# First attention of a two-block transformer: queries as high over low halves in 128 rows, values as high beside low, two matmul passes in place of three

## The chip, the core and the metric

The kernel runs on one core of a Trainium2 chip. Its time is the device time of one execution in microseconds, and the number that counts is the median of several executions. A core has the engines TensorE (PE in the profile: matrix products into PSUM; its weight loads are shown apart as PEld), VectorE (DVE), ScalarE (ACT), GpSimd (POOL) and SyncE (SP, which issues the loads).

## What is computed

Two transformer blocks over 512 tokens of width 1024, all in float32. The first block has two layers; each layer mixes the tokens in three branches (an attention over all tokens, a pooling mixer, an attention over a neighbourhood) and closes with a gated feed-forward part. The second block has a convolution layer and a layer with dilated attention. The change is in the first branch, the attention over all tokens, which occurs once in each of the two layers of the first block:

```python
def global_axial_attention(q, k, v, gq, gk):
    ...
    q = rmsnorm(q.reshape(B, S, A_HEADS, HEAD_DIM), gq)        # 8 heads of 64
    k = rmsnorm(k.reshape(B, S, A_KV_HEADS, HEAD_DIM), gk)     # 2 heads of 64
    v = v.reshape(B, S, A_KV_HEADS, HEAD_DIM)
    q = rope_2d(q, row, col) * (HEAD_DIM ** -0.5)
    k = rope_2d(k, row, col)
    ...
        s = jnp.einsum('bqkgd,bskd->bkgqs', qi, k).astype(jnp.float32)
        p = jax.nn.softmax(s, axis=-1)
        return jnp.einsum('bkgqs,bskd->bqkgd', p.astype(v.dtype), v)
```

## The kernel before

All large products are made in a float32 form (`F32R`) that TensorE streams in one pass but that keeps fewer bits. Each operand is therefore split into a high part (a copy rounded to that form, made on ACT) and a low part (the operand minus the high part, made on DVE), and a product is three passes into one PSUM tile: high by high, high by low, low by high (`mm3`, lines 325 to 327, for the weights; `split_out`, lines 671 and 672, makes the two parts). The weights stream from memory in units of eight 128x128 tiles (`raw`, line 270) and are split on the chip two units ahead of their use (lines 295 and 296).

A layer of the first block begins with `mixer`. In its first stage the projections of the pooling branch, of k, of v and of the four pairs of query heads run one after the other (`pool_inputs`, `axial_inputs`), and what follows each projection runs beside the next ones. For k and each q that is `rope`: squares on ACT (`rsq`, line 739), a scaled copy on ACT (`rqg`, line 740), small sums on PE (`qks`, line 744), a rotation on PE (`rot`, line 749), a short chain of 128x8 operations on DVE (`qkv`, `nwa`, `qky`), a product on POOL (line 755), and on DVE `rrs` (line 757) and the sum into `rqg` (line 759). Then the parts are made: `kh` and `kl`, `qh` and `ql`. Before, `k` of head e (of two) stands in its own 64 partitions of a 128-partition tile whose other 64 are zero, so that `qh[:, i]`, which holds two heads one above the other, can be multiplied whole; `vh` and `vl` likewise have zeros in the other head's 64 columns.

The second stage is `axial_lane`: two lanes take sixteen units (a pair of heads i, half of the tokens u, a head e of the pair). A unit makes two score tiles of 128 queries by 512 keys (`sc`, lines 862 to 864), a softmax of each (maximum on DVE line 835, exponent on ACT line 842, reciprocal on DVE line 846, scaling on POOL line 847), four transposes of each (`pt`, line 875), a split of the result into `ph` and `pl`, and twelve products of 256 columns with v (`po`, lines 890, 893 and 894: four blocks of keys by three passes). The four units of a pair i add into one `po` tile, which is then split into `yh[:, i]` and `yl[:, i]`. Beside the lanes runs `branch(l, 1, ...)`, the gates (`mm`) and output products (`z`) of the pooling branch. After the stage the neighbourhood attention begins.

What stands next to what on an engine is decided when the program is made: each lane says how long it will wait (`AX_NEXT`, `AX_SOFTMAX`, `AX_PROB`), `spend` advances a clock with each piece of PE work, `tick` lets a lane go on when its time has come, and the layer below moves single instructions among each other. Each engine then works through its list in order. PSUM has eight tiles: three for `mm`/`z`, three (tag `a`) that `sc`, `pt` and `rot` share, two (tag `b`) for `po`, `qks` and others.

Of the kernel before, what the change touches and what calls it, by code (L numbers as in the profile page):

```python
# [226 lines left out]
class Kernel:  # L227
# [534 lines left out]
    def axial_inputs(self, l):  # L762
# [4 lines left out]
        vh = self.ap.tile([P, 4, 2, P], F32R, tag="vh", name="vh")  # L767
        vl = self.ap.tile([P, 4, 2, P], F32R, tag="vl", name="vl")
        qh = self.ap.tile([P, 4, S], F32R, tag="qh", name="qh")
        ql = self.ap.tile([P, 4, S], F32R, tag="ql", name="ql")  # L770
        rq = self.ap.tile([P, 4, 8], F32, tag="rq", name="rq")
        zero = self.rp.tile([P, S], F32, tag="wide", name="zero")
        nc.gpsimd.memset(zero, 0.0)
        none = zero[:, :256].rearrange("p (i d) -> p i d", i=4)
        for v in (vh, vl):
            nc.scalar.activation(v[:, :, 0, 64:], none, AF.Copy)
            nc.scalar.activation(v[:, :, 1, :64], none, AF.Copy)
        for k in (kh, kl):
            nc.scalar.activation(k[64:, 0], zero[64:], AF.Copy)
            nc.scalar.activation(k[:64, 1], zero[:64], AF.Copy)  # L780
        done = [False] * 4

        def on_k(ps):
# [13 lines left out]
            for e, r in ((0, slice(0, 64)), (1, slice(64, P))):  # L797
                nc.scalar.activation(kh[r, e], qg[r], AF.Copy)
                nc.vector.tensor_tensor(kl[r, e], qg[r], kh[r, e].bitcast(F32), op=OP.subtract)

        def on_v(ps):
# [8 lines left out]
            self.split_out(vh[:, :, 0, :64], vl[:, :, 0, :64], pt[:, :, :64])  # L810
            self.split_out(vh[:, :, 1, 64:], vl[:, :, 1, 64:], pt[:, :, 64:])

        def on_q(ps, i):
            qg, y = yield from self.rope(ps, self.vec(f"qk_norm_q{l}"))
            self.split_out(qh[:, i], ql[:, i], qg)
# [11 lines left out]
        return jobs, (kh, kl, vh, vl, qh, ql, rq), done  # L827
# [21 lines left out]
    def axial_lane(self, units, st, tiles, y):  # L849

        nc = self.nc
        kh, kl, vh, vl, qh, ql, rq = tiles
        yh, yl = y
        while units:
            i, u, e = units.popleft()
# [3 lines left out]
            for t in (2 * u, 2 * u + 1):  # L859
                cols = slice(t * P, (t + 1) * P)  # L860
                ps = self.psum("a", "sc")
                nc.tensor.matmul(ps, qh[:, i, cols], kh[:, e], start=True, stop=False)
                nc.tensor.matmul(ps, qh[:, i, cols], kl[:, e], start=False, stop=False)
                nc.tensor.matmul(ps, ql[:, i, cols], kh[:, e], start=False, stop=True)
                self.spend(0.65)
# [15 lines left out]
            if i not in st:  # L881
                st[i] = self.psum("b", "po")
                st[i, "n"] = 0
# [13 lines left out]
            if st[i, "n"] == 4:  # L897
                self.split_out(yh[:, i], yl[:, i], po)
# [783 lines left out]
```

## Time and profile before

| | |
|---|---|
| median of 3 runs | 3252.92 us (3252.04 to 3722.86) |
| the profiled execution | 3250.97 us |
| its span, first to last instruction | 3249.2 us |
| PE busy | 3157.3 us, 97% |
| DVE busy | 1783.0 us, 55% |
| ACT busy | 1329.3 us, 41% |
| mean granted TensorE clock | 0.992 of full speed |

The profile is of one execution. Busy times of PE count a product until its result has left the array, so products overlap in the list: what one costs is the distance from its start to the start of the next. The chain of waits is followed back from the last instruction and tells which engine held the end up. The stage of `axial_lane` lies from 91 to 223 us in the first layer and from 940 to 1072 us in the second.

### The profile page before, as it was taken

To read this page: it belongs to the slowest core of one execution; us is meant where nothing else is said; L and a number is where in the kernel's file an instruction comes from. 1 tells how busy PE (TensorE), PEld (TensorE's weight loads), DVE (VectorE), ACT (ScalarE), POOL (GpSimd) and SP (SyncE) were. 2 spreads that over 40 slices of the span, in tenths; PEclk is the share of its full clock that TensorE was granted. 3 is DMA by queue.
4 is the path that set the end of the run, shared out by engine and by line. 5 is a ranking of instruction groups with operands and counts; after the bars stand their busy time and mean duration, and the time that the engine had idled before them with its cause. 6 is when DMAs were issued, how large, how long until landed. Compare 5 with 4: busy or idle time off the path is not lost.

```text
span 3249.2 us, 41363 instructions
## 1 busy us (share of the span) xinstructions
PE 3157.3 (97%) x16172; PEld 2664.2 (82%) x16172; DVE 1783.0 (55%) x3187; ACT 1329.3 (41%) x2160; POOL 493.7 (15%) x448
## 2 busy tenths in 40 slices
PE   8999999999999999999999989999899999999998
PEld 7887888888888788888879868888788888888886
DVE  6668446456675753645465356446634454464555
ACT  5456334334444643434343154334333333353332
POOL 0113110000111322000005410000433334100001
PEclk9999999999999999999999989999999999999999
DMA  3112232222221222232232222222222222222221
GB/s 141 59 61 74 98 111 79 97 100 94 91 69 53 77 87 101 84 104 96 95 108 77 67 80 71 98 97 104 84 72 79 77 78 79 79 85 98 97 98 72
DMA packets 86403, 281.80 MB, mean 87 GB/s; under 512 B 11584, under 2 KB 17984, under 8 KB 86208
## 3 DMA queue, kind: packets, MB, share of 16 engines
q1 hardware_dynamic: 85632, 278.10, 24.7%
q8 instruction: 128, 2.10, 0.3%
q10 hardware_dynamic: 576, 1.05, 0.1%
q14 instruction: 67, 0.55, 0.1%
HBM read 274.91 MB, written 2.10 MB: 85 GB/s over the span
## 4 chain that ended last, share of the span: by engine, by line
PE 87%; DVE 8%; ACT 4%; issue 1%; DMA 0%; POOL 0%; SPq 0%; DVEq 0%; ACTq 0%; POOLq 0%
PE mm L327 18%; PE mm L326 18%; PE mm L325 18%; PE mm L511 6%; PE mm L512 6%; PE mm L513 6%; PE conv L1264 2%; ACT junk L382 2%; PE z L327 1%; PE z L326 1%; PE z L325 1%; DVE w L296 1%; PE htp L444 1%; PE pt L875 1%; PE dpo L1398 1%
## 5 line engine op out<-in xcount | busy, mean ns | idle before, releaser
L325 PE MATMUL mm<-hh,w 128*128 128x512 f32 (+1 forms) x2720 | 1052.7, 387 | 0.0
L326 PE MATMUL mm<-hl,w 128*128 128x512 f32 (+1 forms) x2720 | 1035.2, 381 | 0.0
L327 PE MATMUL mm<-hh,w 128*128 128x512 f32 (+1 forms) x2720 | 1035.0, 381 | 0.0
L296 DVE TENSOR_TENSOR w<-raw,w 128x1024 fp32r<-128x1024 f32 x436 | 567.8, 1302 | 465.7 <-ACT w L295 461.0
L327 PEld LDWEIGHTS mm<-hh,w 128*128 128x128 f32 x2720 | 511.8, 188 | 96.5 <-issue 1.2
L326 PEld LDWEIGHTS mm<-hl,w 128*128 128x128 f32 x2720 | 512.6, 188 | 90.4 <-issue 2.4
L325 PEld LDWEIGHTS mm<-hh,w 128*128 128x128 f32 x2720 | 512.3, 188 | 90.2 <-issue 1.9
L295 ACT ACTIVATE w<-raw 128x1024 fp32r<-128x1024 f32 x436 | 459.0, 1053 | 247.7 <-PE mm L513 187.0
L403 POOL TENSOR_TENSOR y<-y,row 128x512 f32<-128x512 f32 x40 | 54.3, 1389 | 1311.1 <-ACT junk L382 1311.1
L625 DVE SCALAR_TENSOR_TENSOR cg<-mm,vecs,cg 128x511 f32<-128x511 f32 (+1 forms) x176 | 131.9, 749 | 212.8 <-ACT cg L618 209.9
L292 POOL TENSOR_TENSOR raw<-raw,vecs 128x1024 f32<-128x1024 f32 x72 | 145.5, 2021 | 562.2 <-DMA raw<-in_wall 558.2
L512 PE MATMUL mm<-w,ah 128*128 128x512 f32 x576 | 226.5, 393 | 0.0
L511 PE MATMUL mm<-w,ah 128*128 128x512 f32 x576 | 225.7, 392 | 0.0
L513 PE MATMUL mm<-w,al 128*128 128x512 f32 x576 | 225.7, 392 | 0.0
L625 DVE SCALAR_TENSOR_TENSOR cv<-mm,vecs,cv 128x511 f32<-128x511 f32 (+1 forms) x176 | 131.9, 750 | 100.2 <-ACT cv L618 97.3
L618 ACT ACTIVATE cg<-mm,vecs 128x512 f32<-128x512 f32 x88 | 68.7, 781 | 286.3 <-PE mm L327 286.1
L326 PE MATMUL mm<-hl,keep 128*128 128x256 f32 x512 | 143.4, 282 | 7.0 <-DVE hl L675 6.9
L327 PE MATMUL mm<-hh,keep 128*128 128x256 f32 x512 | 142.9, 281 | 0.1
L325 PE MATMUL mm<-hh,keep 128*128 128x256 f32 x512 | 142.1, 284 | 0.2 <-ACT hh L674 0.2
L511 PEld LDWEIGHTS mm<-w,ah 128*128 128x128 f32 x576 | 109.1, 189 | 23.5 <-issue 0.8
L513 PEld LDWEIGHTS mm<-w,al 128*128 128x128 f32 x576 | 109.1, 189 | 22.6
L512 PEld LDWEIGHTS mm<-w,ah 128*128 128x128 f32 x576 | 109.1, 189 | 22.4
(287 smaller groups left out, 4552.8 us busy)
## 6 DMA issues: line engine op xcount, KB each, us to landing
raw<-in_wall SPq DMA_DIRECT2D x500, 512.0 KB, 3.2
row<-in_rows SPq DMA_DIRECT2D x9, 512.0 KB, 4.1
x<-in_x SPq DMA_DIRECT2D x4, 512.0 KB, 6.1
bt<-in_rpb SPq DMA_DIRECT2D x16, 128.0 KB, 2.1
cup<-cu SPq DMA_DIRECT2D x128, 16.0 KB, 1.8
out<-x SPq DMA_DIRECT2D x4, 256.0 KB, 2.1
out<-x ACTq DMA_DIRECT2D x4, 256.0 KB, 2.1
taps<-in_cm_taps SPq DMA_DIRECT2D x1, 576.0 KB, 4.9
```

What stands on the lines that cost most here:

```text
L292: nc.gpsimd.tensor_tensor(rows, rows, g[:, k0 : k0 + n, None].to_broadcast(list(rows.shape)), op=OP.mult)
L295: nc.scalar.activation(hi, raw, AF.Copy)
L296: nc.vector.tensor_tensor(lo, raw, hi.bitcast(F32), op=OP.subtract)
L325: nc.tensor.matmul(ps, wh, xh, start=first and i == 0, stop=False, **check)
L326: nc.tensor.matmul(ps, wh, xl, start=False, stop=False, **check)
L327: nc.tensor.matmul(ps, wl, xh, start=False, stop=stop, **check)
L382: self.nc.scalar.activation(junk, x, AF.Square, accum_out=total)
L511: nc.tensor.matmul(ps, xh, wh, start=first, stop=False)
L512: nc.tensor.matmul(ps, xh, wl, start=False, stop=False)
L513: nc.tensor.matmul(ps, xl, wh, start=False, stop=last)
L618: nc.scalar.activation(o, ps, AF.Identity, scale=self.vec(taps + str(k0), f), bias=self.vec(cb, f))
L625: nc.vector.scalar_tensor_tensor(o[:, to], ps[:, of], self.vec(taps + str(k), f), o[:, to], op0=OP.mult, op1=OP.add,)
```

## The change

In the scores, head e of pair i is taken alone. Its 64 rows of high parts stand in 64 partitions and its low parts in the other 64 (`q[:, i, e]`); `kh` and `kl` hold the same 64 rows of k twice. One pass with `kh` then adds high by high and low by high, and a second one with `kl` the rest, among it low by low, which was left out before. In the products with v the high and low parts of v stand side by side in the columns, so that the pass with `ph` and the one with `pl` give 128 rows, of which 64 belong to the high part and 64 to the low one; at the end of each (i, e) ACT copies one half to a new tile `pot`, DVE adds the other, and the sum is split in 64 partitions. The zeros are no longer written. Units go by (i, e, u), so that both lanes work on one (i, e) and each has its own `po` tile. The core of the diff:

```diff
-        zero = self.rp.tile([P, S], F32, tag="wide", name="zero")
-        nc.gpsimd.memset(zero, 0.0)
...
-        for v in (vh, vl):
-            nc.scalar.activation(v[:, :, 0, 64:], none, AF.Copy)
-            nc.scalar.activation(v[:, :, 1, :64], none, AF.Copy)
-        for k in (kh, kl):
-            nc.scalar.activation(k[64:, 0], zero[64:], AF.Copy)
-            nc.scalar.activation(k[:64, 1], zero[:64], AF.Copy)
+        ends = (slice(0, 64), slice(64, P))
...
-            for e, r in ((0, slice(0, 64)), (1, slice(64, P))):
+            for e in range(2):
+                r, o = ends[e], ends[1 - e]
                 nc.scalar.activation(kh[r, e], qg[r], AF.Copy)
-                nc.vector.tensor_tensor(kl[r, e], qg[r], kh[r, e].bitcast(F32), op=OP.subtract)
+                nc.scalar.activation(kh[o, e], qg[r], AF.Copy)
+                for to in (r, o):
+                    nc.vector.tensor_tensor(kl[to, e], qg[r], kh[r, e].bitcast(F32), op=OP.subtract)
...
-            self.split_out(vh[:, :, 0, :64], vl[:, :, 0, :64], pt[:, :, :64])
-            self.split_out(vh[:, :, 1, 64:], vl[:, :, 1, 64:], pt[:, :, 64:])
+            self.split_out(v[:, :, 0, :64], v[:, :, 0, 64:], pt[:, :, :64])
+            self.split_out(v[:, :, 1, 64:], v[:, :, 1, :64], pt[:, :, 64:])
...
-            self.split_out(qh[:, i], ql[:, i], qg)
+            for e in range(2):
+                r, o = ends[e], ends[1 - e]
+                nc.scalar.activation(q[r, i, e], qg[r], AF.Copy)
+                nc.vector.tensor_tensor(q[o, i, e], qg[r], q[r, i, e].bitcast(F32), op=OP.subtract)
...
-                nc.tensor.matmul(ps, qh[:, i, cols], kh[:, e], start=True, stop=False)
-                nc.tensor.matmul(ps, qh[:, i, cols], kl[:, e], start=False, stop=False)
-                nc.tensor.matmul(ps, ql[:, i, cols], kh[:, e], start=False, stop=True)
-                self.spend(0.65)
+                nc.tensor.matmul(ps, q[:, i, e, cols], kh[:, e], start=True, stop=False)
+                nc.tensor.matmul(ps, q[:, i, e, cols], kl[:, e], start=False, stop=True)
+                self.spend(0.45)
...
-                nc.tensor.matmul(
-                    po[:, cols], vh[:, k, e], a, start=st[i, "n"] == 0 and k == 0, stop=False, **check
-                )
-                nc.tensor.matmul(po[:, cols], vh[:, k, e], b, start=False, stop=False, **check)
-                nc.tensor.matmul(po[:, cols], vl[:, k, e], a, start=False, stop=k == 3, **check)
-            self.spend(1.3)
-            st[i, "n"] += 1
-            if st[i, "n"] == 4:
-                self.split_out(yh[:, i], yl[:, i], po)
+                nc.tensor.matmul(
+                    po[:, cols], v[:, k, e], a, start=st[i, e, "n"] == 0 and k == 0, stop=False, **check
+                )
+                nc.tensor.matmul(po[:, cols], v[:, k, e], b, start=False, stop=k == 3, **check)
+            self.spend(0.95)
+            st[i, e, "n"] += 1
+            if st[i, e, "n"] == 2:
+
+                r, o = (slice(0, 64), slice(64, P)) if e == 0 else (slice(64, P), slice(0, 64))
+                t = self.xp.tile([P, S], F32, tag="pot", name="pot", bufs=2)
+                nc.scalar.activation(t[r], po[o], AF.Copy)
+                nc.vector.tensor_tensor(t[r], t[r], po[r], op=OP.add)
+                self.split_out(yh[r, i], yl[r, i], t[r])
...
-                    units = deque((i, u, e) for i in range(4) for u in range(2) for e in range(2))
+                    units = deque((i, e, u) for i in range(4) for e in range(2) for u in range(2))
```

The order of the rest moves with it, in and just before the stage of the lanes; behind the first two products after the stage, the order of PE's products is the same as before up to the next such stage, and to the end of the program.

The first place is PE's list at the end of the first layer's stage of lanes, from the last score pass of the last unit to the third of its four groups of transposes. `mm` is the first projection of the neighbourhood attention, which follows the stage. Before:

```order
L864 MATMUL sc<-kh,ql 128x512
L326 MATMUL mm<-hl,w_1892 128x512
L327 MATMUL mm<-hh,w_1892 128x512
L325 MATMUL mm<-hh,w_1892 128x512
L326 MATMUL mm<-hl,w_1892 128x512
L327 MATMUL mm<-hh,w_1892 128x512
L875 MATMUL pt<-ident,pm 128x128 x4
L325 MATMUL mm<-hh,w_1892 128x512
L326 MATMUL mm<-hl,w_1892 128x512
L875 MATMUL pt<-ident,pm 128x128 x4
L327 MATMUL mm<-hh,w_1892 128x512
L875 MATMUL pt<-ident,pm 128x128 x4
```

With the change:

```order
L861 MATMUL sc<-kl,q 128x512
L327 MATMUL mm<-hh,w_1842 128x512
L325 MATMUL mm<-hh,w_1842 128x512
L326 MATMUL mm<-hl,w_1842 128x512
L872 MATMUL pt<-ident,pm 128x128 x4
L327 MATMUL mm<-hh,w_1842 128x512
L325 MATMUL mm<-hh,w_1842 128x512
L326 MATMUL mm<-hl,w_1842 128x512
L327 MATMUL mm<-hh,w_1842 128x512
L872 MATMUL pt<-ident,pm 128x128 x4
L325 MATMUL mm<-hh,w_1842 128x512
L872 MATMUL pt<-ident,pm 128x128 x4
```

Behind the last score pass stand now nine products `mm` and three groups of `pt` ahead of the fourth group; before, there were eleven `mm` and three groups. The last three score tiles followed each other without a gap before; now each of them stands alone, with `po` or `mm` between.

The second place is ACT's list ahead of the first exponent (`pm`) of the first layer; `qh_631` and `q_630` are the tiles of the queries, `rqg_867` and `rqg_863` hold the third pair of query heads, `rqg_929` and `rqg_927` the fourth, `rsq_928` its squares. Before:

```order
L671 ACTIVATE qh_631<-rqg_805 128x512
L740 ACTIVATE rqg_867<-mm_808,vecs_75 128x512
L295 ACTIVATE w12_1045<-raw12_989 128x1024
L671 ACTIVATE qh_631<-rqg_867 128x512
L739 ACTIVATE rsq_928<-mm_870 128x512
L740 ACTIVATE rqg_929<-mm_870,vecs_75 128x512
L295 ACTIVATE w13_1108<-raw13_1043 128x1024
L671 ACTIVATE qh_631<-rqg_929 128x512
L842 ACTIVATE pm_970,smx_971<-sc_966,smx_971,rq_633 128x512
L842 ACTIVATE pm_981,smx_982<-sc_977,smx_982,rq_633 128x512
L842 ACTIVATE pm_1004,smx_1005<-sc_1000,smx_1005,rq_633 128x512
```

With the change:

```order
L739 ACTIVATE rsq_926<-mm_866 128x512
L812 ACTIVATE q_630<-rqg_863 64x512 x2
L740 ACTIVATE rqg_927<-mm_866,vecs_75 128x512
L295 ACTIVATE w13_1104<-raw13_1039 128x1024
L812 ACTIVATE q_630<-rqg_927 64x512 x2
L1075 ACTIVATE gate_1036<-mm_986,hb_93 128x512
L295 ACTIVATE w14_1200<-raw14_1102 128x1024
L840 ACTIVATE pm_969,smx_970<-sc_966,smx_970,rq_631 128x512
L840 ACTIVATE pm_979,smx_980<-sc_976,smx_980,rq_631 128x512
L840 ACTIVATE pm_1001,smx_1002<-sc_998,smx_1002,rq_631 128x512
L840 ACTIVATE pm_1011,smx_1012<-sc_1008,smx_1012,rq_631 128x512
```

The two copies of the third pair stand now behind the squares of the fourth pair and ahead of its scaled copy `rqg_927`, on which its rotation on PE waits, and the gate and the split of a weight unit (`w14_1200`) have moved ahead of the first exponent.

The third place is DVE's list after the first two units of the first layer, where the softmax of the next four score tiles (`smx<-sc` is the maximum) begins. Before:

```order
L835 TENSOR_REDUCE smx_1133<-sc_1128 128x1
L839 SCALAR_TENSOR_TENSOR smx_1133<-smx_1133,rq_633 128x1
L846 RECIPROCAL smx_1133<-smx_1133 128x1
L835 TENSOR_REDUCE smx_1156<-sc_1151 128x1
L835 TENSOR_REDUCE smx_1167<-sc_1162 128x1
L839 SCALAR_TENSOR_TENSOR smx_1156<-smx_1156,rq_633 128x1
L835 TENSOR_REDUCE smx_1178<-sc_1173 128x1
L839 SCALAR_TENSOR_TENSOR smx_1167<-smx_1167,rq_633 128x1
L839 SCALAR_TENSOR_TENSOR smx_1178<-smx_1178,rq_633 128x1
L846 RECIPROCAL smx_1156<-smx_1156 128x1
L846 RECIPROCAL smx_1167<-smx_1167 128x1
```

With the change:

```order
L833 TENSOR_REDUCE smx_1124<-sc_1120 128x1
L833 TENSOR_REDUCE smx_1147<-sc_1143 128x1
L837 SCALAR_TENSOR_TENSOR smx_1124<-smx_1124,rq_631 128x1
L898 TENSOR_TENSOR pot_1138<-pot_1138,po_1111 64x512
L837 SCALAR_TENSOR_TENSOR smx_1147<-smx_1147,rq_631 128x1
L833 TENSOR_REDUCE smx_1157<-sc_1153 128x1
L844 RECIPROCAL smx_1124<-smx_1124 128x1
L672 TENSOR_TENSOR yl_965<-pot_1138,yh_964 64x512
L837 SCALAR_TENSOR_TENSOR smx_1157<-smx_1157,rq_631 128x1
L833 TENSOR_REDUCE smx_1170<-sc_1166 128x1
L844 RECIPROCAL smx_1147<-smx_1147 128x1
```

Between the maxima stand now the sum `pot` and the low part `yl` of the finished (i, e); before, a `yl` stood there after every second pair of units, and no `pot`.

## Rows read from the trace of the kernel before

**Rows 1.** The page: busy times of the engines, and the chain that ended last
```profile
PE 3157.3 (97%) x16172; PEld 2664.2 (82%) x16172; DVE 1783.0 (55%) x3187; ACT 1329.3 (41%) x2160; POOL 493.7 (15%) x448
...
PE 87%; DVE 8%; ACT 4%; issue 1%; DMA 0%; POOL 0%; SPq 0%; DVEq 0%; ACTq 0%; POOLq 0%
```

**Rows 2.** Busy time in stretches: us, then PE, PEld, DVE, ACT, POOL, clock, DMA
```profile
80.00:100.00 20.00, 18.76 (x86) 14.44 (x85) 18.04 (x62) 8.66 (x16) 5.55 (x4) 1.00 0.20 74
100.00:120.00 20.00, 20.00 (x109) 17.18 (x108) 11.18 (x24) 10.29 (x19) 4.18 (x6) 1.00 0.15 53
```

**Rows 3.** Groups by line and form: count, then busy us, mean ns, idle before
```profile
L864 PE MATMUL sc<-kh,ql 128*128 128x512 f32 x64 | 25.2, 394 | 0.0
...
L894 PE MATMUL po<-ph,vl 128*128 128x256 f32 x128 | 36.1, 282 | 0.0
```

**Rows 4.** Instructions in order of time, PE: start us, duration us, line, operation
```profile
198.11 0.28 PE L890 MATMUL po<-ph,vh 128*128 128x256 f32 x1
...
199.55 0.39 PE L862 MATMUL sc<-kh,qh 128*128 128x512 f32 x1
...
200.25 0.39 PE L862 MATMUL sc<-kh,qh 128*128 128x512 f32 x1
```

**Rows 5.** The same view, PE around the transposes, at 103 and 208 us
```profile
102.96 1.04 PE L875 MATMUL pt<-ident,pm 128*128 128x128 f32 x8
...
104.06 0.39 PE L326 MATMUL mm<-hl,w 128*128 128x512 f32 x1
...
208.07 0.60 PE L875 MATMUL pt<-ident,pm 128*128 128x128 f32 x4
...
208.75 0.39 PE L862 MATMUL sc<-kh,qh 128*128 128x512 f32 x1
```

**Rows 6.** Instructions of the tiles kl, qh, wot: ns min/median/max, first and last start
```profile
L799 DVE TENSOR_TENSOR kl<-rqg,kh x4: 683/686/1674, 72.8 to 922.2; 64x512 fp32r<-64x512 f32 x4
...
L671 ACT ACTIVATE qh<-rqg x8: 632/632/635, 77.2 to 945.2; 128x512 fp32r<-128x512 f32 x8
...
L1050 DVE TENSOR_TENSOR wot<-wot,wpo x16: 678/686/692, 258.0 to 1179.6; 64x512 f32<-64x512 f32 x16
```

**Rows 7.** The chain of waits in order of time, first layer: start us, us, what
```profile
79.60 0.60 DVE ql L672
...
88.02 0.63 ACT qh L671
...
94.61 0.50 PE sc L862
```

**Rows 8.** Instructions in order of time, both layers, with [idle before, what ended it]
```profile
90.28 0.17 DVE L753 TENSOR_SCALAR qkv<-qks 128x8 f32<-128x8 f32 x1 [0.53 <-PE qks L744]
...
91.75 2.18 POOL L755 TENSOR_TENSOR rqg<-rqg,cos 128x512 f32<-128x512 f32 x1 [5.18 <-PE rot L749]
...
92.71 1.25 DVE L353 SCALAR_TENSOR_TENSOR qky<-nwa,qky 128x8 f32<-128x8 f32 x1
...
94.61 0.50 PE L862 MATMUL sc<-kh,qh 128*128 128x512 f32 x1 [0.88 <-DVE rrs L757]
...
926.11 0.17 DVE L753 TENSOR_SCALAR qkv<-qks 128x8 f32<-128x8 f32 x1 [1.15 <-PE qks L744]
...
933.34 0.17 DVE L753 TENSOR_SCALAR qkv<-qks 128x8 f32<-128x8 f32 x1 [1.04 <-PE qks L744]
```

**Rows 9.** The same view at the end of the first layer's lanes
```profile
209.21 0.40 PE L864 MATMUL sc<-kh,ql 128*128 128x512 f32 x1
...
212.15 0.69 POOL L847 TENSOR_SCALAR pm<-pm,smx 128x512 f32<-128x512 f32 x1 [5.97 <-DVE smx L846]
...
215.72 0.63 PE L875 MATMUL pt<-ident,pm 128*128 128x128 f32 x4 [0.16 <-ACT pm L842]
```

**Rows 10.** Busy time in a stretch of the convolution layer, columns as in Rows 2
```profile
2310.00:2350.00 40.00, 30.89 (x205) 28.37 (x204) 29.55 (x43) 15.55 (x29) 16.79 (x10) 0.88 0.28 93
```

**Rows 11.** Who waited for whom on PE: us in total, times, longest
```profile
PE ltp L1185 <- DVE vt L1306: 9.1, 1, 9.1
```

More of the change, by code (lines that the diff above doesn't have):

```diff
@@ L766, in axial_inputs @@
         kl = self.ap.tile([P, 2, S], F32R, tag="kl", name="kl")
[L767 to L770, printed above, removed]
+        v = self.ap.tile([P, 4, 2, P], F32R, tag="v", name="v")
+        q = self.ap.tile([P, 4, 2, S], F32R, tag="q", name="q")
         rq = self.ap.tile([P, 4, 8], F32, tag="rq", name="rq")
-        zero = self.rp.tile([P, S], F32, tag="wide", name="zero")
-        nc.gpsimd.memset(zero, 0.0)
-        none = zero[:, :256].rearrange("p (i d) -> p i d", i=4)
-        for v in (vh, vl):
-            nc.scalar.activation(v[:, :, 0, 64:], none, AF.Copy)
-            nc.scalar.activation(v[:, :, 1, :64], none, AF.Copy)
-        for k in (kh, kl):
-            nc.scalar.activation(k[64:, 0], zero[64:], AF.Copy)
-            nc.scalar.activation(k[:64, 1], zero[:64], AF.Copy)
+        ends = (slice(0, 64), slice(64, P))
         done = [False] * 4
@@ L826, in axial_inputs @@
             jobs.append((gemm_tiles("w_in", l, [T_Q + i], range(KD)), lambda ps, i=i: on_q(ps, i)))
-        return jobs, (kh, kl, vh, vl, qh, ql, rq), done
+        return jobs, (kh, kl, v, q, rq), done
     def softmax_rows(self, ps, scale_col, scale, pmat, mx=None):
@@ L851, in axial_lane @@
         nc = self.nc
-        kh, kl, vh, vl, qh, ql, rq = tiles
+        kh, kl, v, q, rq = tiles
         yh, yl = y
         while units:
-            i, u, e = units.popleft()
+            i, e, u = units.popleft()
             while not st["ready"][i]:
@@ L880, in axial_lane @@
                 yield AX_PROB
-            if i not in st:
-                st[i] = self.psum("b", "po")
-                st[i, "n"] = 0
-            po = st[i]
+            if (i, e) not in st:
+                st[i, e] = self.psum("b", "po")
+                st[i, e, "n"] = 0
+            po = st[i, e]
             cols = slice(2 * u * P, (2 * u + 2) * P)
```

## The prediction, made before the changed kernel was run

> **What bounds the kernel now.** I read the page first: PE is busy for 97% of the span, and 87% of the chain that ended last is PE, 8% DVE, 4% ACT [rows 1]. So a product taken off PE's list shortens the kernel where PE has no gap, and new work on DVE or ACT lengthens it only in the few places where the chain leaves PE. The second view is busy time in stretches: in the stage of the lanes PE is full (20.00 of 20 us between 100 and 120 us), while DVE and ACT are at 11.18 and 10.29; just before, between 80 and 100 us, PE has 18.76 and DVE 18.04 [rows 2]. The third is the chain itself: in the first layer it leaves PE and runs through DVE (`ql` at 79.60 us) and ACT (`qh` at 88.02 us) until `sc` takes it up again at 94.61 us [rows 7]. So the place to fear is the start of the stage, where k and q are prepared.
>
> **What is removed.** The order of the changed program has 192 products less: one `sc` pass of 512 columns for each of 64 score tiles and one `po` pass of 256 columns of 128 [rows 3]. The mean durations there (394 and 282 ns) overlap; what counts is the distance between starts. Three `sc` passes go from 199.55 to 200.25 us, so one is 0.233 us; twelve `po` passes from 198.11 to 199.55 us, so one is 0.120 us [rows 4]. 64 x 0.233 = 14.9 us and 128 x 0.120 = 15.4 us: 30.3 us, all in a stage without a gap on PE. The remaining passes keep shape and type; the rows that held zeros now hold numbers, which I cost at nothing, since the zero rows streamed as well. The removed writes of zeros lie on ACT and POOL beside products and give nothing.
>
> **What the order adds on PE.** In about six pairs of units of each layer the two groups of eight transposes become four groups of four. Eight with the product behind them take 104.06 - 102.96 = 1.10 us, four 208.75 - 208.07 = 0.68 us [rows 5]; without the product (0.23 us) that is 0.87 and 2 x 0.45 = 0.90 us. So a split costs 0.03 us, and 12 pairs x 2 splits 0.7 us.
>
> **The start of the stage.** `kl` gets two more DVE operations per layer and each q one more, of 0.69 us in 64 partitions just as in 128 [rows 6]. Up to the fourth pair's `rrs`, which frees the PSUM tile that the third score tile waits for (0.88 us already now, at 94.61 us [rows 8]), DVE has five more: 3.4 us. Against this stand 0.5 us in which it was idle at 90.28 us [rows 8] and four `mm` products (0.9 us) that the new order puts ahead of the first `sc`: 2.0 us are left in the first layer. The reordered ACT list is in the same chain: the scaled copy `rqg` of the fourth pair now stands behind two copies of the third, of 0.63 us each [rows 6], which wait for DVE; its rotation on PE and then `rrs` are late next. In the second layer DVE waits for PE twice on the way, 1.15 and 1.04 us [rows 8], and catches up; what stays is ACT's second copy, 0.63 us, ahead of the squares of the fourth pair, which `qks` on PE needs: 0.6 us. Together 2.6 us. Bounds: nothing, if the added operations fall into the pauses of DVE's chain of small operations; and all five with ACT's copy in both layers, 2 x (3.4 + 0.6) = 8.0 us. I stay nearer the lower end, as the first layer alone has its chain there.
>
> **The middle of the stage.** Each finished (i, e) now costs ACT a copy of some 0.6 us (`qh` takes 0.63), DVE a sum of 0.69 us (`wot` is the same operation in the neighbourhood attention [rows 6]) and both a split, where a pair i cost one split. For DVE that is 8 sums, 4 more `yl` and one q, 9 us per layer on about 72 us of the 131 us (11.18 of 20 [rows 2]): 81 us in a stage of 117 us, so it stays below PE. The work that hides them is what stands between scores and transposes, some 6 us of `z` and `mm`.
>
> **The end of the stage.** There this cover is gone. One tile's softmax takes 3.2 us from the end of its last score pass (209.21 + 0.40) to the end of POOL's scaling (212.15 + 0.69), and PE waits already, for 0.16 us and more, at 215.72 us [rows 9]. In the new order nine products and three groups of four stand between the last score pass and the last group: 9 x 0.23 + 3 x 0.45 = 3.4 us, hardly more than 3.2, and `pot` and `yl` (2 x 0.69 us on DVE) and two copies (1.2 us) on ACT stand among the four softmaxes. The pair of units before has fifteen products and three groups there, 4.8 us. I take 1.2 us of new waiting per layer, between nothing and the whole 1.4 + 1.2 us: 2.4 us. What stands behind is the first PSUM read of the next stage on ACT, late by the longer way through `pot`; PE has 55 products in its list before it needs that.
>
> **The sum.** 0.7 + 2.6 + 2.4 - 30.3 = -24.6 us. Against the profiled execution (3250.97 us, 1.8 us more than its span) this gives 3226.4 us; against the median of the runs, 1.95 us higher, 3228.3 us.
>
> **A rule weighed against it.** One `kl` operation took 1674 ns where the middle one took 686 [rows 6], and one of 128x8 elements took 1.25 us during POOL's product of 2.18 us [rows 8]: DVE is held up now and then, while POOL works. The Trainium skill, SBUF — State Buffer, "Who interferes with whom", says why: a VectorE instruction with two SBUF inputs is blocked by a GpSimd instruction that reads SBUF, one with at most one such input isn't. The trace agrees with it as far as these rows go. By the rule the change is worse than its count, since `yl` read PSUM and now reads `pot` in SBUF, during POOL's scaling; it is the second rival below.
>
> **The rivals.**
> - *All of it is gained.* The added work falls into pauses; DVE's 55% and ACT's 41% [rows 1] speak for it, the chain at 79 to 95 us [rows 7] against it. -30.3 us: 3222.6 us.
> - *DVE holds PE up at both ends.* 28 of its new or changed operations have two SBUF inputs. If the five at each start and the two `yl` at each end are each held up by 1.0 us (1674 - 686 [rows 6]), that is 14 us more: -10.6 us, 3242 us. For it speak 18.04 of 20 us at the start [rows 2], against it that PE's weights are split two units ahead.
> - *Slower than before: the clock.* In the convolution layer PE waited once for 9.1 us [rows 11], and in a stretch of 40 us there the granted clock was 0.88 [rows 10], so 0.24 of it ran at 1.2 and not 2.4 GHz and 4.8 us were lost. If start and end of each stage grew waits like that one, 4 x (9.1 + 4.8) = 56 us would be added to -30: 3278 us. It decides from waits of 30 us together. Between 80 and 100 us, with PE's gaps of today, the clock is 1.00 [rows 2].
>
> **How the numbers follow.** The forecast has 0.60, all gained 0.15, DVE 0.20, the clock 0.02, and 0.03 is for what I don't see. The likeliest gives 3228.3 us. The range goes from the first rival with a little of the spread of runs, 3221, to the second, 3242 us. 2% are 65 us, about what a measurement of this kernel can tell from no change; the first three cases lie within it, as more than 30 us can't be gained by 30 us of removed work: faster 0.01, same 0.97, slower 0.02.
>
> **What would show it.** PE with 192 products less and the stage of the lanes about 14 us shorter in each layer, with PE full in its middle: the removal. A wait of the third score tile for `rrs` grown from 0.9 to about 3 us in the first layer, and a short one of the fourth pair's `rot` or `qks`: the start. Waits of `pt` for `pm` of about a microsecond at each end: the end. It is wrong if the pitch of `sc` or `po` passes isn't 0.23 and 0.12 us, if PE waits in the middle of the stage, or if the granted clock falls in it.

## The result, and the profile after

The changed kernel takes 3232.65 us (median of four runs, 3230.66 to 3237.67) where the kernel before took 3252.48 us beside it. The ratio of the means is 0.9944, 95% interval 0.9924 to 0.9963; it leaves out one execution of before, 3722.86 us, that was in a slow state. The medians differ by 19.8 us (19.4 without that execution), against 24.6 us forecast and 30.3 us of removed products. The forecast of 3228.3 us lies 4.4 us too low, and the measured time lies inside the range of 3221 to 3242 us. The profiled execution took 3233.43 us with a span of 3231.6 us, near the median.

The page of the changed kernel (busy times, chain that ended last), which answers to [rows 1]:

```profile
PE 3135.7 (97%) x15980; PEld 2641.5 (82%) x15980; DVE 1806.9 (56%) x3223; ACT 1347.7 (42%) x2180; POOL 497.0 (15%) x446
...
PE 85%; DVE 9%; ACT 4%; issue 1%; DMA 0%; POOL 0%; SPq 0%; DVEq 0%; ACTq 0%; POOLq 0%
```

PE has 192 instructions less and is 21.6 us less busy; DVE has 23.9 us more and a slightly larger share of the chain. Busy time in stretches of the first layer's lanes, against [rows 2] (columns as there):

```profile
80.00:100.00 20.00, 17.58 (x80) 13.30 (x79) 19.42 (x58) 8.48 (x13) 3.97 (x3) 1.00 0.24 80
...
140.00:160.00 20.00, 20.00 (x113) 17.24 (x112) 12.42 (x26) 10.87 (x20) 3.56 (x4) 1.00 0.17 54
180.00:200.00 20.00, 19.68 (x112) 16.30 (x111) 14.01 (x27) 13.38 (x25) 4.08 (x6) 1.00 0.16 54
200.00:220.00 20.00, 19.70 (x107) 16.07 (x106) 15.02 (x29) 13.88 (x25) 4.17 (x6) 1.00 0.23 79
```

The last two stretches of the kernel before:

```profile
180.00:200.00 20.00, 20.00 (x113) 17.19 (x112) 10.16 (x21) 9.12 (x17) 2.74 (x4) 1.00 0.15 53
200.00:220.00 20.00, 19.84 (x114) 16.35 (x113) 13.31 (x33) 11.67 (x26) 5.58 (x8) 1.00 0.08 27
```

The middle is full on PE, as before. At the start PE is down from 18.76 to 17.58 of 20 us while DVE is up from 18.04 to 19.42, and at the end PE is idle for 0.3 us in each stretch, where before it was idle for 0.0 and 0.2 us. The granted clock stays at 1.00 in all of them.

Where PE waits in these stages, in order of time, first layer (four lines) and start of the second (two). The line of `sc` in the first layer answers to the wait of 0.88 us in [rows 8], that in the second layer to one of 0.89 us before. The waits of `rot` and of `qks` in the second layer have no counterpart before; ahead of `pt` PE waited once in each layer before, for 0.2 us:

```profile
92.42 1.12 PE L749 MATMUL rot<-rqg,rot 128*128 128x512 f32 x2 [1.03 <-ACT rqg L740]
...
97.03 0.50 PE L860 MATMUL sc<-kh,q 128*128 128x512 f32 x1 [1.39 <-DVE rrs L757]
...
196.27 0.66 PE L872 MATMUL pt<-ident,pm 128*128 128x128 f32 x4 [0.31 <-POOL pm L845]
...
206.98 0.66 PE L872 MATMUL pt<-ident,pm 128*128 128x128 f32 x4 [0.29 <-POOL pm L845]
...
927.52 1.05 PE L744 MATMUL qks<-heads,rsq 128*128 128x2 f32 x8 [1.21 <-ACT rsq L739]
...
932.95 0.50 PE L860 MATMUL sc<-kh,q 128*128 128x512 f32 x1 [0.87 <-DVE rrs L757]
```

**A ledger along PE's list.** Waits don't sum up to the missing 5 us, so I put the two traces side by side: each has 12,576 `mm` products, and the n-th of one can be set against the n-th of the other (the expectations count up to 32 products less for the same places). At `mm` product 257 (49.93 us before, ahead of the first stage) the changed kernel was 0.46 us behind, at product 807 (287.11 us, behind the first lanes) 11.43 us ahead: the first stage gave 11.9 us. From product 3463 (907.77 us) to 3863 (1096.31 us), around the second lanes, it went from 12.76 to 23.81 us: 11.1 us. So both stages together gave 22.9 us, 1.7 us less than forecast. From product 3863 to 12432 (3203.34 us) 6.3 us of it went again, in parts of the program where all engines have the same instructions in the same order as before the change. More than half of that, 3.4 us, went between products 9063 and 10663 (2366.74 to 2814.15 us), the heads of the fourth layer's attention.

The same ledger for all traces of this study, each against the first trace of before (us; minus is a gain; "at 1.2" is the time between products 3863 and 12432 in which the granted clock was 1.2 and not 2.4 GHz, summed over the clock records of the trace; "landing" is the median time from issue to landing of the 512 KB weight units, "dwb" PE's seven waits of `dwb` for DVE's `dw` in the fourth layer):

| kernel | time | 257 to 807 | 3463 to 3863 | 3863 to 12432 | of it 9063 to 10663 | at 1.2 | landing | dwb |
|---|---|---|---|---|---|---|---|---|
| before, first trace | 3250.97 | 0 | 0 | 0 | 0 | 37.5 | 3.2 | 2.5 |
| before, second | 3249.44 | -0.5 | 0.0 | -1.6 | 0.0 | 30.7 | 3.2 | 2.4 |
| before, third | 3252.92 | -0.1 | 0.0 | +2.9 | +0.1 | 44.4 | 3.2 | 2.6 |
| changed, first | 3233.43 | -11.9 | -11.1 | +6.3 | +3.4 | 44.4 | 3.6 | 5.1 |
| changed, second | 3231.48 | -11.5 | -11.1 | +1.4 | +2.9 | 37.5 | 3.6 | 5.3 |
| changed, third | 3234.42 | -11.8 | -11.1 | +4.8 | +4.8 | 41.0 | 3.6 | 5.1 |
| 192 left out (e1_less) | 3225.39 | -13.5 | -13.4 | +1.7 | +2.9 | 37.5 | 3.6 | 4.9 |
| scores only | 3244.72 | -5.6 | -4.8 | +1.2 | +0.1 | 41.0 | 3.3 | 2.5 |
| values only | 3244.89 | -4.8 | -4.6 | +0.7 | +0.5 | 41.0 | 3.2 | 2.9 |
| q on POOL | 3238.49 | -7.7 | -8.0 | +4.1 | +3.6 | 41.0 | 3.6 | 4.9 |
| `kl` on ACT | 3233.78 | -10.8 | -10.3 | +2.2 | +2.6 | 37.5 | 3.6 | 4.6 |
| later q | 3234.86 | -12.7 | -11.3 | +7.8 | +4.3 | 47.8 | 3.6 | 5.4 |
| no `pot` | 3228.78 | -12.7 | -11.8 | +1.5 | +2.9 | 34.1 | 3.7 | 4.9 |
| products added (e4_pad) | 3237.11 | -11.8 | -10.7 | +4.6 | +0.1 | 51.2 | 3.2 | 2.5 |

The times are those of the profiled executions. The stages repeat within 0.5 us where the same kernel was traced again, while the part behind them moves by several us.

Much of that movement is the granted clock. Between products 9063 and 10663 it was 1.00 in all traces; the rest of the part behind the stages was shortest, by 1.6 us, in the second trace of before, with 30.7 us at 1.2 GHz, and longest, by 4.5 us, with the added products, with 51.2 us. At one place the first and second traces of the changed kernel, in this order, show it after the same wait of PE for 2.48 us; product by product the second gained 1.5 us there (the second pair of lines has busy times and, third from the end, the clock):

```profile
2817.47 2.01 PE L511 MATMUL mm<-keep,dyh 128*128 128x512 f32 x6 [2.48 <-ACT keep L295]
...
2817.03 1.65 PE L511 MATMUL mm<-keep,dyh 128*128 128x512 f32 x6 [2.48 <-ACT keep L295]
...
2817.00:2824.00 7.00, 6.53 (x22) 5.23 (x23) 4.10 (x5) 3.37 (x4) 0.00 (x0) 0.76 0.56 183
...
2816.60:2823.60 7.00, 6.57 (x28) 5.36 (x29) 4.11 (x5) 3.34 (x4) 0.00 (x0) 1.00 0.56 182
```

### The profile page after: what moved, and what is told of

The parts are those of the page before. It is cut to its first block, busy times and chain, and to the rows that moved or that the text cites. A ratio compares the mean times of both kernels' runs of the same rounds, so it can differ in the third digit from the quotient of the medians.

```text
span 3231.6 us, 41019 instructions
## 1 busy us (share of the span) xinstructions
PE 3135.7 (97%) x15980; PEld 2641.5 (82%) x15980; DVE 1806.9 (56%) x3223; ACT 1347.7 (42%) x2180; POOL 497.0 (15%) x446
## 4 chain that ended last, share of the span: by engine, by line
PE 85%; DVE 9%; ACT 4%; issue 1%; DMA 0%; POOL 0%; SPq 0%; DVEq 0%; ACTq 0%; POOLq 0%
PE mm L327 18%; PE mm L326 18%; PE mm L325 18%; PE mm L512 6%; PE mm L513 6%; PE mm L511 6%; PE conv L1265 2%; ACT junk L382 2%; DVE w L296 1%; PE z L325 1%; PE z L326 1%; PE z L327 1%; PE htp L444 1%; PE pt L872 1%; PE dpo L1399 1%
```

## The experiments

**The changed kernel again**, no edit.

> The changed kernel once more, for a second trace of it. In the first trace the stage of the lanes is 11.9 us shorter in the first layer and 12.4 us in the second, measured between `mm` products that stand on both sides of it, against 11.6 and 13.0 forecast, and 6.2 us are given back later, between 1796 and 1955 us and between 2299 and 2800 us, although from the end of the second stage on all engines have the same instructions in the same order as before. Theory A, scatter: how DVE's small operations meet POOL's scaling of weights there differs from execution to execution; the stages repeat within 0.3 us, the part behind differs from the first trace by more than 1 us. Theory B, a consequence of the shorter stage: the part behind it repeats too, 6 us longer than before within 1 us.

Measured: 3232.74 us (3231.48 to 3234.68), ratio 0.9938 (0.9925 to 0.9950). The stages repeat (11.5 and 11.1 us); the part behind them gave back 1.4 and not 6.3 us. So much of it is scatter, as the second and third traces of before also show below; but not all, since the heads of the fourth layer gave back 2.9 us again. The 12.4 us that the expectation names for the second layer go from product 807 to 3863 and so hold 1.3 us that the first trace gained between the stages; around the second lanes alone it is 11.1 us.

**The removed products alone** (the diff of the `po` part is alike: the line with `vl` goes):

```
-                nc.tensor.matmul(ps, qh[:, i, cols], kl[:, e], start=False, stop=False)
-                nc.tensor.matmul(ps, ql[:, i, cols], kh[:, e], start=False, stop=True)
+                nc.tensor.matmul(ps, qh[:, i, cols], kl[:, e], start=False, stop=True)
```

> The kernel before with the 192 products left out and nothing else changed: the third `sc` pass (low part of q with the high part of k) and the third `po` pass (low part of v). The order of all other instructions stays. It prices the removed passes alone. My theory, passes at 0.233 and 0.120 us on a full PE: each stage 15.1 us shorter, 30.3 us in both, and the median near 3222 us if nothing is given back behind the stages. Rival, what hides softmax and transposes gets too short without them: up to 3 us per stage of new waits of `pt` for `pm`, so 24 to 28 us. Behind the stages: 6 us given back if that is what any shorter stage does, between 0 and 6 if it is scatter.

Measured: 3227.83 us, ratio 0.9922 (0.9910 to 0.9935). The stages are 13.5 and 13.4 us shorter, not 15.1. Against the expectation the order did not stay: with shorter score tiles the layer below put the fourth one of each pair of units earlier, and it now waits for a PSUM tile, which the kernel before did at one pair in each layer. PE and ACT of this kernel in order of time:

```profile
173.07 0.78 ACT L842 ACTIVATE pm<-sc,smx,rq 128x512 f32<-128x512 f32 x1 [3.21 <-DVE smx L839]
...
173.69 0.39 PE L325 MATMUL mm<-hh,w 128*128 128x512 f32 x1
...
173.99 0.50 PE L862 MATMUL sc<-kh,qh 128*128 128x512 f32 x1
174.33 0.39 PE L863 MATMUL sc<-kl,qh 128*128 128x512 f32 x1
```

The fourth tile needs one of three buffers and gets that of the first, when ACT's exponent has read it (173.07 + 0.78 = 173.85); the fourth tile begins 0.14 us after that, here and, within 0.01 us, at six pairs in each layer. The gaps of 0.30 and 0.34 us in place of 0.23 cost 0.18 us for this pair of units: two units take 15.94 us there, where 17.63 - 1.89 = 15.74 were expected. The six pairs of the first layer lose 1.2 us more than before in this way, of the missing 1.6 us. The waits of `pt` for `pm` that the rival named aren't there.

**The score half alone.** From the kernel before, with the new k and q and:

```
+                nc.tensor.matmul(ps, q[:, i, e, cols], kh[:, e], start=True, stop=False)
+                nc.tensor.matmul(ps, q[:, i, e, cols], kl[:, e], start=False, stop=True)
```

> Only the score half of the change: queries high over low, both halves of k doubled, two `sc` passes; values, their three `po` passes, the order of the units and the single sum per pair stay as before. My theory: 14.9 us of passes less, 2.6 us for the start of the stages: 12.3 us faster, 3240 us, with PE's waits of `rot`, `qks` and the third `sc` at the start as in the changed kernel and none of `pt` at the end beyond those of before. Rival, the doubled preparation on DVE is what costs, held up by POOL: 3 us and more at each start, so 9 us or less.

Measured: 3245.10 us, ratio 0.9974 (0.9964 to 0.9985), 7.9 us faster; the stages 5.6 and 4.8 us shorter, of 7.5 us removed in each. The waits at the start are those of the changed kernel (`rot` 1.00 us, third `sc` 1.73 us; `qks` 0.15 and 1.20 us in the second layer), none of `pt` at the end. So the losses at the start belong to this half; 1.8 and 2.6 us are lost, between my 1.3 per layer and the rival's 3.

**The value half alone.** From the kernel before, with the new v, the order by heads, two `po` passes and `pot`.

> Only the value half: hi beside lo of v, two `po` passes, order of units by head, the sum over two halves of `po` through `pot`; queries, k and the three `sc` passes stay. My theory: 15.4 us of passes less, 0.7 us for the split groups of transposes, 2.4 us for the end: 12.3 us faster, 3240 us, waits of `pt` for `pm` at the end of each stage and a start as before. Rival, the end costs nothing as the third `sc` pass still covers the softmax: 14.7 us faster, 3238 us.

Measured: 3245.31 us, ratio 0.9976 (0.9968 to 0.9985), 7.7 us faster; the stages 4.8 and 4.6 us shorter, of 7.7 removed. Neither theory had this: 3 us per layer are lost, with a start as before. Where PE waited in the first layer of this kernel (90 to 240 us; total, times, longest):

```profile
PE cvp L951 <- DVE cvt L945: 1.3, 1, 1.3
PE sc L857 <- DVE rrs L757: 0.9, 1, 0.9
PE pt L870 <- ACT pm L837: 0.4, 1, 0.4
```

The largest loss is a wait of the next stage's transposes `cvp` for DVE's copy `cvt`, the last of a row of DVE operations that begins with the last `pot` and `yl`. The changed kernel doesn't have this wait; why its list avoids it stays open. So the halves don't add up: -5.6 and -4.8 in the first layer, but -11.8 together.

**q's high part on POOL.**

```
-                nc.scalar.activation(q[r, i, e], qg[r], AF.Copy)
+                nc.gpsimd.tensor_copy(q[r, i, e], qg[r])
```

> The changed kernel with the high part of q (two copies of 64x512 for each pair) made on POOL and not on ACT. In the changed kernel these copies wait on ACT for DVE's sum into `rqg` and stand ahead of the squares and the scaled copy of the next pair; between matched products the start of the stage costs about 2.0 us in the first layer and 2.7 us in the second, with waits of `rot` (1.03 us) and `qks` (1.21 and 0.17 us) for ACT. Theory A, ACT's order is the cause: these waits go, the second layer's stage gets 1.5 us shorter, the first one's by up to 1 us. Theory B, DVE and POOL get in each other's way: POOL's copies are in front of its product with `cos` and beside DVE's subtractions; then the wait of the third `sc` for `rrs` grows by 2 us or more and the stages get longer.

Measured: 3238.10 us, ratio 0.9958 (0.9945 to 0.9971), by its median slower than the changed kernel, though the intervals overlap; the stages show it, with 7.7 and 8.0 us gained only. Theory B: ACT's waits are gone, but `rrs` comes later in both layers (the `sc` tile that waits for it, in the first and the second layer):

```profile
96.92 0.79 PE L860 MATMUL sc<-kh,q 128*128 128x512 f32 x1 [3.94 <-DVE rrs L757]
...
938.65 0.50 PE L860 MATMUL sc<-kh,q 128*128 128x512 f32 x1 [4.15 <-DVE rrs L757]
```

POOL does hold DVE up there: between 86 and 95 us two of q's subtractions take 1.08 and 1.64 us, where the changed kernel's take 0.69, and four operations of 128x8 take 0.56 to 1.15 us and end within 0.03 us of a copy or product of POOL.

**`kl`'s second copy on ACT.**

```
-                for to in (r, o):
-                    nc.vector.tensor_tensor(kl[to, e], qg[r], kh[r, e].bitcast(F32), op=OP.subtract)
+                nc.vector.tensor_tensor(kl[r, e], qg[r], kh[r, e].bitcast(F32), op=OP.subtract)
+                nc.scalar.activation(kl[o, e], kl[r, e].bitcast(F32), AF.Copy)
```

> The changed kernel with the second copy of the low part of k (two of the four `kl` operations of a layer) made by ACT from the first one, not by a second subtraction on DVE: two DVE operations of 0.69 us less, two ACT operations of 0.63 us more at each start. If DVE's additional operations carry the cost of the first layer's start, as the prediction has it, the wait of the third `sc` for `rrs` falls by about 1.4 us to nothing and the stage is 1 us shorter or more. If it is ACT's order, the wait stays and the stage is no shorter.

Measured: 3234.39 us, ratio 0.9941 (0.9929 to 0.9954), no faster than the changed kernel. In the first layer the wait for `rrs` falls to nothing, as the theory of DVE's operations has it, but the stage is 1.1 us longer, with a new wait of PE for the squares of the fourth pair (PE, then ACT, DVE and POOL):

```profile
93.07 1.05 PE L744 MATMUL qks<-heads,rsq 128*128 128x2 f32 x8 [2.21 <-ACT rsq L739]
...
91.11 1.28 ACT L812 ACTIVATE q<-rqg 64x512 fp32r<-64x512 f32 x2 [4.00 <-DVE rqg L759]
92.42 0.60 ACT L739 ACTIVATE rsq<-mm 128x512 f32<-128x512 f32 x1
...
87.11 2.38 DVE L813 TENSOR_TENSOR q<-rqg,q 64x512 fp32r<-64x512 f32 x2
...
85.93 2.29 POOL L755 TENSOR_TENSOR rqg<-rqg,cos 128x512 f32<-128x512 f32 x1 [2.77 <-PE rot L749]
```

The wait is put down to ACT, but ACT sat idle for 4.00 us for DVE ahead of it. Two things moved with the edit. The squares of the fourth pair stand now behind the third pair's copies also in the first layer, where the changed kernel has them ahead; and one of the second pair's subtractions took 1.66 us beside POOL's product, where none of the changed kernel's took over 0.69. So the run can't price the two operations taken off DVE: the order and the hold-up by POOL changed as well.

**The parts of q later in the planner's order.**

```
             qg, y = yield from self.rope(ps, self.vec(f"qk_norm_q{l}"))
+            yield 4.5
             for e in range(2):
```

> The changed kernel with a pause of 4.5 us of the planner's clock between the rotation and the parts of q. In ACT's list of the first layer the scaled copy of the fourth pair now stands ahead of the third pair's two copies; in the second layer the squares of the fourth pair still stand behind them. ACT's order as the cause: the wait of `rot` (1.03 us) goes in the first layer, and `qks` in the second still waits 1.2 us. Rival: the wait only moves on to `rrs`, and the stage's length is unchanged within 0.2 us.

Measured: 3233.24 us, ratio 0.9940 (0.9927 to 0.9954). The wait of `rot` in the first layer is gone, that of the third `sc` has grown to 2.38 us, and the stage is 0.8 us shorter than in the first trace of the changed kernel (12.7 against 11.9), more than the rival allowed; the second layer, where the order didn't change, still has `qks` waiting for 1.45 us and gains 0.2 us. ACT's order is thus worth 0.8 of some 2 us in the first layer. In the median nothing of it can be told from the changed kernel.

**Without `pot`**, in place of a copy, a sum and a split of the sum:

```
+                self.split_out(yh[r, i], yl[r, i], po[r])
```

> The changed kernel without the sum of the two halves of `po`: the copy on ACT and the addition on DVE for each head are left out, and `yh` and `yl` are made from one half alone. It prices `pot`. At the end of each stage the changed kernel has about 1.0 us more idle time than before the change, with two waits of `pt` for `pm` of 0.3 us. If `pot` and the longer way behind it are the cause, 0.5 to 1.0 us per layer come back; if it is the shorter cover (two `sc` and eight `po` passes where there were three and twelve), nothing does. The middle of the stages, 15.8 us for two units, stays as it is in both.

Measured: 3230.67 us, ratio 0.9933 (0.9921 to 0.9946). The stages are 0.8 and 0.7 us shorter than in the changed kernel's first trace, the second of the two waits of `pt` at each end is gone, and two units in the middle still take 15.81 us. So `pot` costs nothing in the middle and most of the end's loss.

**The kernel before, two more traces, and the changed one, a third.**

> The kernel before, for a second trace of it. Behind the second stage, from `mm` product 3780 to 12400, all kernels have the same instructions in the same order; nine traces of changed kernels took there between 0.7 and 7.6 us more than the one trace of before. If that is scatter, other traces of before take 1 to 7 us more than its first one too, here and in the next run. If it is a consequence of the change, they repeat the first one within 0.5 us. The stages themselves repeat within 0.3 us in both.

> The kernel before, for a third trace: as in the run ahead of it. Scatter: the part behind the stages lies 1 to 7 us over the first trace, and not at the same value as in the second. A consequence of the change: within 0.5 us of the first.

> The changed kernel, for a third trace. Its first two took 6.3 and 1.5 us more behind the stages than the first trace of before. Scatter: any value from 0 to 7 us; the stages again 11.7 us (first layer) and 11.1 us (second) shorter within 0.3 us.

Measured: in before the part behind the stages lies 1.6 us under and 2.9 us over the first trace, so scatter of that size is its own; with 30.7, 37.5 and 44.4 us at 1.2 GHz the three traces stand in the same order. Between 1697 and 1709 us, for one, the first trace had a mean clock of 0.86 and the second of 1.00, behind the same wait of 2.8 us, and the second was 1.5 us shorter. But neither theory is the whole: between products 9063 and 10663, where the clock was 1.00 in all, the three traces of before agree within 0.2 us, and the three of the changed kernel lie 2.9 to 4.8 us over them. There POOL multiplies each weight unit by a gain as it lands, beside DVE's chain for `dw`. That place in the first trace of the changed kernel, with before's below it:

```profile
2396.46 1.90 POOL L292 TENSOR_TENSOR raw<-raw,vecs 128x1024 f32<-128x1024 f32 x1 [5.68 <-DMA raw<-in_wall]
...
2397.70 0.67 DVE L1443 TENSOR_TENSOR dw<-dmx,one 128x4 f32<-128x4 f32 x1
```

```profile
2417.07 1.90 POOL L292 TENSOR_TENSOR raw<-raw,vecs 128x1024 f32<-128x1024 f32 x1 [5.29 <-DMA raw<-in_wall]
...
2418.70 0.28 DVE L1442 TENSOR_TENSOR dw<-dmx,one 128x4 f32<-128x4 f32 x1
```

DVE's operation of four columns ends with POOL's product in both (2396.46 + 1.90 = 2398.36 and 2417.07 + 1.90 = 2418.97, against 2398.37 and 2418.98). In the changed kernel POOL began 0.39 us later in relation to DVE, because the weights landed later, and PE's `dwb` waits so much longer (0.73 us, before 0.36). The Trainium skill, SBUF — State Buffer, "Who interferes with whom", says that a VectorE instruction with two SBUF inputs contends with a GpSimd instruction that reads SBUF. This pair of rows agrees with it. The lists of DMA issues, changed kernel and then before (512 KB units, median us to landing):

```profile
raw<-in_wall SPq DMA_DIRECT2D x500, 512.0 KB, 3.6
```

```profile
raw<-in_wall SPq DMA_DIRECT2D x500, 512.0 KB, 3.2
```

Nothing in the change touches these transfers, and they are slower already between 60 and 200 us, 3.6 against 3.2 us. Over all traces the slow landing goes with 192 products less and not with the chip: scores alone (64 less) and values alone (128 less) have 3.3 and 3.2 us.

**The changed kernel with 192 products added again**, of 2x2 numbers, where PE waits for the input:

```
+                for _ in range(192):
+                    nc.tensor.matmul(pad[:2, :2], self.pads[:, :2], self.pads[:, 2:4], start=True, stop=True)
```

> The changed kernel with 192 products of 2x2 numbers added on PE ahead of its first transposes, where it waits for the input anyway (until 13.5 us); their result is never read. With them PE has as many products as before the change. In all traces so far a weight unit of 512 KB lands 3.2 to 3.3 us after its issue in the kernels with at most 128 products less (before three times, scores alone, values alone) and 3.6 to 3.7 us in all with 192 less, from 50 us on, ahead of the first changed instruction too; and where POOL scales these units beside DVE's chain for `dwb`, PE waits 2.0 to 2.9 us in the former and 4.6 to 5.4 us in the latter. If the number of products is what sets the landing (as a matter of where program and weights lie in memory), units land after 3.2 us again, `dwb` waits 2 to 3 us, and the part behind the second stage, from product 3780 to 12400, takes up to 2 us more than in the first trace of before, where the changed kernel had 1.5 to 6.3 us more; the median is near 3230 us or lower, if the added products cost nothing. If something else sets it, the landing stays at 3.6 us, `dwb` waits 5 us, and the median stays near 3233 us.

Against the expectation PE doesn't have as many products as before: each of the 192 stands twice in the trace, so that PE has 16364 instructions, 384 more than the changed kernel and 192 more than before:

```profile
L1546 PE MATMUL pad<-pads x384: 164/164/166, 1.1 to 16.0; 128*2 128x2 f32 x192
```

Measured: landing at 3.2 us, and in the waits of the fourth layer (2300 to 2850 us), this kernel and then the changed one:

```profile
PE dwb L358 <- DVE dw L1451: 2.5, 7, 0.6
```

```profile
PE dwb L358 <- DVE dw L1451: 5.1, 7, 1.0
```

Between products 9063 and 10663 it takes 0.1 us more than before, where the changed kernel took 2.9 to 4.8 more. So the slower landing costs 2.9 to 4.8 us there, and it went when products were added to the same kernel. That the number of products sets it is the likeliest reading, not shown: the run also starts its first `mm` 4.5 us later, and there is no trace of the changed kernel without the additions on this chip; against the chip speaks that the changed kernel and its versions had 3.6 to 3.7 us on all others. The kernel as a whole isn't faster, 3235.83 us (3228.90 to 3239.12), ratio 0.9939 (0.9925 to 0.9953): the added products end only at 16.2 us, and behind the stages the profiled execution lost 4.5 us outside those heads, with more time at 1.2 GHz than any other trace. Whether a longer program is worth it without the late start stays open, as does how the landing can follow the program's size; that it lies in where program and weights are placed wasn't tested. No version that computes everything is faster than the changed kernel by more than the runs scatter.

## Why the prediction was right, and where it wasn't

**The removed passes** were sized right. In the middle of the stage two units begin 15.80 us apart, 1.83 us less than before (17.63); four `sc` and eight `po` passes are 4 x 0.233 + 8 x 0.12 = 1.89 us. First `po` of two such pairs of the changed kernel:

```profile
156.52 0.28 PE L887 MATMUL po<-ph,v 128*128 128x256 f32 x1
...
172.32 0.28 PE L887 MATMUL po<-ph,v 128*128 128x256 f32 x1
```

**The split transposes** fit too: the missing 0.06 us per pair of units are as much as two splits of 0.03 us. **The middle of the stage** stays full on PE, and 16 copies and sums of `pot` are hidden there, as said (no `pot`: the same 15.81 us).

**The start** is the term that was mis-sized. From the ledger at product 470 (first layer), where twelve `sc` and sixteen `po` passes are gone (4.7 us), 2.6 us had been gained: 2.1 us lost, 2.0 without the splits, just what the prediction took. That is in part luck: it took them from DVE's five operations, as a wait of the third `sc` of 3 us; that wait grew only to 1.39 us, and another 1.03 us stands in ACT's order (`rot`), as the later q shows. In the second layer, at product 3640, 2.0 us of 4.7 had been gained: 2.7 us lost, 2.6 without the splits, where 0.6 us was forecast. Not all of this is preparation: with the products left out and nothing else changed, 4.3 and 4.2 us had been gained at these places, so 0.4 and 0.6 us were lost there as well. The step that failed is "In the second layer DVE waits for PE twice on the way [...] and catches up; what stays is ACT's second copy". By the prediction's own numbers five operations of 0.69 us don't fit into 1.15 and 1.04 us. DVE didn't catch up: the two pauses of [rows 8] are gone, and one of 0.36 us is left in front of the fourth pair. DVE, then ACT, second layer of the changed kernel:

```profile
928.61 0.17 DVE L753 TENSOR_SCALAR qkv<-qks 128x8 f32<-128x8 f32 x1 [0.36 <-PE qks L744]
```

```profile
925.56 1.28 ACT L812 ACTIVATE q<-rqg 64x512 fp32r<-64x512 f32 x2 [4.01 <-DVE rqg L759]
926.87 0.60 ACT L739 ACTIVATE rsq<-mm 128x512 f32<-128x512 f32 x1
```

ACT sits idle for 4.01 us ahead of the third pair's copies, which wait for DVE, and the squares of the fourth pair stand behind them. So `qks` was late by DVE's lateness and by the second copy, not by the copy alone: five operations, 3.4 us, less the pauses, 2.2 us, plus the copy, 0.6 us, would have given 1.8 us, against 2.0 us measured (2.6 less 0.6). My bounds (up to 4.0 us in each layer) held it.

**The end** was right in size: of 15.15 us 11.8 and 11.1 us were gained; without start and splits that leaves about 1.1 us per layer, forecast 1.2. It shows as two waits of 0.3 us and short gaps, not as one of a microsecond, and `pot` is 0.7 to 0.8 of it.

**The rivals.** Not all was gained. That DVE's new operations would be held up by POOL at both ends fell for the changed kernel: `yl` from `pot` took 674 to 779 ns and q's subtractions 684 to 689 ns, and only one `kl` took 1687 ns, as one did before. POOL's products with `cos` do hold up one small operation of DVE each at the start, for 1.2 to 1.3 us in place of 0.2, but in both kernels alike (in the first layer of before at 78, 85 and 93 us, of the changed one at 80, 86 and 94 us). One row of before goes against the rule as the prediction words it: `qky<-qkv`, with one input, took 1.26 us at 934.56 us beside such a product. What differs between the kernels is the hold-up in the fourth layer, of which the prediction has no term. The clock stayed at 1.00 in the stage.

**What the sum left out** is the rest of the program. The stages gave 22.9 us, 1.7 less than 24.6. Of the other 3.1 us to the median's 19.8, the slower landing of the weights takes 2.9 to 4.8 us in the fourth layer. The scatter of the rest behind the stages (-1.6 to +2.8 us in before alone) covers what remains; it goes largely with the time at 1.2 GHz and is no consequence of the change that these traces could show.

## What to carry to other kernels

Where two traces differ by less than their waits explain, put the n-th product of one against the n-th of the other: stages that repeat within half a microsecond can be judged one by one, although the whole scatters by several. A pause of an engine counts as room for new work once, and what then comes behind an engine's waiting instruction in its list is late as well: sum the new operations against the pauses of each stage rather than assume that it catches up. And an edit that takes an operation off one engine can move the order of others: the `kl` run took two off DVE and got a longer stage, so look at what moved before a wait is put down to an engine's load.

## What the runs showed of the hardware

The landing of a 512 KB weight unit took 3.2 to 3.3 us in the programs with the products of before (or up to 128 less) and 3.6 to 3.7 us in those with 192 less, in all traces of this study and on several chips, and 3.2 us in the one run where products without use were added. In a kernel where POOL works on what has landed and DVE works beside it, these 0.4 us went with 2.6 to 4.8 us of PE's time.

At POOL's products with `cos` in the start of the stages of before and of the changed kernel an operation of DVE on 128x8 elements ended 0.02 or 0.03 us after POOL's and took up to 1.30 us.

After one and the same wait of PE, 2.48 us, the mean granted clock of the next 7 us was 0.76 in one execution of the changed kernel (part of it at 1.2 GHz) and 1.00 in another (2.4 GHz all along). Such places, and not the stages, make most of the difference between executions of one kernel here.
